# Encoder layer on one core: the first token group's finished rows go to memory and are normed in later chunks; its difference forms are made in the output projection and loaded in order of use; row loads are spread over the side steps

## The chip, the core and the metric

The kernel runs on one core of a Trainium2 chip. The metric is the device time of one execution in microseconds, as the median of several runs. The engines are TensorE (PE, with its weight loads as PEld), VectorE (DVE), ScalarE (ACT), GpSimd (POOL) and SyncE (SP), which here only issues DMAs. Each works through its own list of instructions in order.

## The reference

One encoder layer for 1536 tokens (512 of `x_prompt`, 1024 of `x_sample`), D = 1024, D_FF = 4096, all float32:

```python
x = x + merged @ w_out                        # output projection
h2 = rms_norm(x, g_mlp)
x = x + jnp.square(jax.nn.relu(h2 @ w_up)) @ w_down
return rms_norm(x, g_final)
```

`merged` is the gated sum of dilated-window attention and of a spatial-gating unit. That part comes first and the change doesn't touch it.

## The kernel before

Tokens lie in 12 tiles of 128. A float32 matrix product is made of three matmuls over values split in two: `split` (L149 to L151) has ScalarE cast the high part (`hi`, or `hf` and `act` for stationary and moving operands) and VectorE subtract it for the low part (`lo`). Weights come by SP's DMA into `raw` tiles of 256 KB and are split so.

*Output projection* (L757 to L787). For each half `ch` of the columns and each tile t: 24 matmuls with w_out, VectorE adds the result to x1[t] (L773), ScalarE sums squares (L231). In the second half x1[t] is also stored to `x1_scr` (SP, L776), `rstd_of` (L211 to L222) makes the root by nine small VectorE operations, two L782 scale the row to h, and in the midst of the next tile's matmuls `h_features` transposes h on TensorE (L741), multiplies by g_mlp on VectorE into `h2T` (L743, two buffers), and SP stores h2T to `h2_scr` (L746).

*MLP.* Two groups g of 6 tiles each (768 tokens, in two halves of HT = 384). Products are done by a scheme of seven block products, called forms: p1, p2 and q4 use blocks as they are, q3, q5, q6, q7 sums or differences of blocks. A group has CH = 8 chunks of the hidden dimension. A chunk has two `up_products` (j = 0, 1: seven forms of 12 matmuls 128x384, L883, in the order UP_ORDER = p1, q6, q7, p2, q5, q4, q3; p2 goes on in p1's PSUM bank and q3 in q5's) with the squared relu, and one `down_products` (seven forms, three tiles each, matmuls 128x512, L933), which adds into the rows x[0..5]. I call the 168 matmuls L883 of a chunk its up product and the 126 matmuls L933 its down product. In an up product ScalarE copies p1's bank to `p` (L888), and VectorE makes `v` = q6 - p (L891). In a down product `held["p", t]` (tag p, 3 buffers) and `z` (tag z, 2 buffers) hold such sums; L949 and L950 add z into rows on GpSimd, L952 adds q5, L956 p2 and L958 q3 on VectorE, and L960 adds p on GpSimd after q3.

The group's forms of h2 are four slabs `hf[k]`. Group 0's are made at the MLP's start: 16 parts loaded from `h2_scr` (L1067), 16 sums on VectorE and 28 splits, k after k. Group 1's difference forms are made as side steps in chunks 1 to 4 of group 0 (`diff_steps`) and stored to `form_scr`; all 28 are loaded as `raw_form` and split (`form_steps`) in group 0's last chunk. Side steps are small pieces of such work; `Side` pops one after each form of a product.

At the MLP's start and after the first up product of group 1, `load_rows` has GpSimd load the six row tiles x from `x1_scr` (L1052, 512 KB each). In that first up product of group 1, group 0's rows are finished by `final_steps(..., spread=True)`: 12 squares on ScalarE (L231), the root, 12 scalings on ScalarE (L1038), 12 multiplications by g_final on GpSimd (L1039), 12 stores to the outputs on GpSimd (L1040). Group 1's rows are normed on VectorE (`normed`, L234) at the very end.

A framework's scheduler writes each engine's list from the program's order and its own estimates, and adds the waits that dependences and reused buffers need. So the place of an instruction is seen only in the built program.

Of the kernel before, what the change touches and what calls it, by code (L numbers as in the profile page):

```python
# [46 lines left out]
SUM_ROWS = 8  # L47
EARLY = 2
DIFFS = ("q3", "q5", "q6", "q7")
UP_ORDER = ("p1", "q6", "q7", "p2", "q5", "q4", "q3")  # L50
# [56 lines left out]
def encoder_kernel(ctx: ExitStack, tc: tile.TileContext, a):  # L107
# [25 lines left out]
    gate_scr = [dram.tile([P, NTOK], F32, name=f"gate_scr{m}") for m in range(EARLY)]  # L133
    form_scr = dram.tile([len(DIFFS), 4, P, HT], F32, name="form_scr")
    h2_scr = dram.tile([KB, P, NTOK], F32, name="h2_scr")
# [118 lines left out]
    with ExitStack() as ph:  # L254
# [3 lines left out]
        vs = vpool.tile([P, NT, DM], F32, name="vs")  # L258
        vparts = const.tile([P, 2 * 32], F32, name="vparts")[:, :2 * NT].rearrange("p (t i) -> p t i", i=2)

# [475 lines left out]
    def h_features(t, halves):  # L736

        for i, h in enumerate(halves):
            pt = tp_tile()
            for b in range(4):  # L740
# [7 lines left out]
                in_=hT2.rearrange("p (k t) -> p k t", k=4))  # L748

    for ch in range(2):  # L750
        cols = slice(ch * 512, (ch + 1) * 512)
# [11 lines left out]
        for t in range(NT):  # L763
            acc = acc_tile()
            terms = token_terms(hT[t // 4], t, lambda k: tuple(x[:, 0, :] for x in w[k]))
            steps = product_steps(acc, [terms[k] for k in w])
            for _ in range(HSTEP):
                next(steps)
            if late:
                h_features(*late)  # L770
            for _ in steps:
                pass
            nc.vector.tensor_add(x1[t][:, cols], x1[t][:, cols], acc)  # L773
            square_sum(x_parts[t][:, ch:ch + 1], x1[t][:, cols], pp)
            if ch:
                nc.sync.dma_start(out=x1_scr[t * P:(t + 1) * P, :], in_=x1[t])  # L776
                rstd = rstd_of(x_parts[t])
                hs = []
                for i in range(2):
                    cs = slice(i * 512, (i + 1) * 512)  # L780
                    h = pp.tile([P, 512], F32, tag="h2", name="h2", bufs=2)
                    nc.vector.tensor_scalar(h, x1[t][:, cs], rstd, None, op0=ALU.mult)  # L782
                    hs.append(h)
                late = t, hs
        if late:
            h_features(*late)
# [128 lines left out]

    def down_products(act, c, x, ending):

        held = {}
        for form in ("p1", "q4", "q6", "q7", "q5", "p2", "q3"):
            w = [  # L920
# [43 lines left out]

    def diff_steps(k):

        x = {}

        def load(key, r, s):
            x[key] = unit("diff")  # L970
            nc.sync.dma_start(out=x[key], in_=h2_scr[4 * s + k, :, GT + r * HT:GT + (r + 1) * HT])

        def store(form, key):
            nc.sync.dma_start(out=form_scr[DIFFS.index(form), k], in_=x[key])

        def first():
            load("a", 0, 0)
            load("b", 1, 0)
            nc.vector.tensor_sub(x["a"], x["a"], x["b"])
            store("q7", "a")  # L980

        def second():
            load("c", 1, 1)
            nc.vector.tensor_sub(x["b"], x["b"], x["c"])
            store("q5", "b")

        def third():
            nc.vector.tensor_add(x["c"], x["a"], x["c"])
            store("q6", "c")

        def fourth():
            load("d", 0, 1)
            nc.vector.tensor_sub(x["d"], x["d"], x["c"])
            store("q3", "d")

        return [first, second, third, fourth]

    def form_source(form, k):
        if form in DIFFS:
            return form_scr[DIFFS.index(form), k]  # L1000
        r, s = {"p1": (0, 0), "p2": (0, 1), "q4": (1, 1)}[form]
        return h2_scr[4 * s + k, :, GT + r * HT:GT + (r + 1) * HT]

    def form_steps(fs):

# [3 lines left out]
        def step(i):  # L1009
            for j in range(i, min(i + 4, len(items))):  # L1010
                if j not in raws:
                    raws[j] = unit("raw_form")
                    nc.sync.dma_start(out=raws[j], in_=form_source(*items[j]))
            form, k = items[i]
# [3 lines left out]

    def final_steps(g, x, tiles, g_final, spread):

# [11 lines left out]
        def rows(j, i):  # L1032
            scale = found["rstd"][:, j:j + 1]
            r = x[tiles[j]][:, i * 512:(i + 1) * 512]
            y = y_rows[6 * g + tiles[j]][:, i * 512:(i + 1) * 512]
            gf = g_final[i]
            if spread:
                nc.scalar.activation(r, r, AF.Copy, scale=scale)  # L1038
                nc.gpsimd.tensor_mul(r, r, gf)  # L1039
                nc.gpsimd.dma_start(out=y, in_=r)  # L1040
            else:
                normed(r, r, scale, gf)
                (nc.scalar, nc.sync)[i].dma_start(out=y, in_=r)
# [4 lines left out]
    def load_rows(g):  # L1048
        x = {}
        for t in (3, 4, 5, 0, 1, 2):  # L1050
            x[t] = mp.tile([P, DM], F32, tag="x", name="x", bufs=6)
            nc.gpsimd.dma_start(out=x[t], in_=x1_scr[(6 * g + t) * P:(6 * g + t + 1) * P, :])  # L1052
        return x

    def gains():
        g_final = [mp.tile([P, 512], F32, tag="z", name="g_final", bufs=2) for i in range(2)]
        for i in range(2):
            load_g(g_final[i], a["g_final"][i * 512:(i + 1) * 512])
        return g_final


    hf = {k: Forms("hf") for k in (3, 0, 1, 2)}
    for k in range(4):
        parts = {}
        for s, r in ((0, 0), (0, 1), (1, 1), (1, 0)):
            parts[r, s] = unit(f"h{r}{s}")
            nc.sync.dma_start(out=parts[r, s], in_=h2_scr[4 * s + k, :, r * HT:(r + 1) * HT])  # L1067
        hf[k].put("p1", parts[0, 0])
        s2 = hf[k].sums(parts[0, 0], parts[1, 0], parts[1, 1])
        hf[k].put("q4", parts[1, 1])  # L1070
        hf[k].last(parts[0, 1], s2)
    x = None
    CH = DFF // P // 4
    for g in range(2):
        for c in range(CH):
            act = []
            final = c == CH - 1
            if g and not c:
                side.add([lambda: None] * 2 + final_steps(0, x, (3, 4, 5, 0, 1, 2), gains(), True))
            for j in range(2):  # L1080
                act.append(Forms("act"))
                if not g and final and j:
                    side.add(form_steps(hf))
                up_products(hf, 2 * c + j, act[j], lambda form: side(1 + (not c)))
            if not c:
                side.flush()
                x = load_rows(g)
            if not g and 1 <= c <= 4:
                side.add(diff_steps(c - 1))
            ending = None  # L1090
            if g and final:
# [3 lines left out]
                def ending(form, t):  # L1095
                    tiles = (3, 4, 5) if (form, t) == ("q5", 2) else (t,) if form == "q3" else ()
                    if tiles:
                        side.add(final_steps(1, x, tiles, [wide[:, :512], wide[:, 512:]], False))
                        side.flush()

            down_products(act, c, x, ending)
            if not g and final:
# [26 lines left out]
```

## Time and profile before

| | |
|---|---|
| median of 3 runs | 2782.21 us (2781.27 to 2785.49) |
| profiled execution | 2783.46 us, span 2781.7 us, mean granted TensorE clock 0.987 |
| busy: TensorE, VectorE, ScalarE, GpSimd | 2681.2 (96%), 1731.4 (62%), 1296.4 (47%), 392.3 us (14%) |
| DMA | 373.57 MB, 134 GB/s over the span |
| first matmul of the MLP, of group 1, last matmul's end | 1771.31, 2269.96, 2765.77 us |

Times in the rows are microseconds from the span's start. Where a row has an idle time in brackets, the arrow names who ended it.

### The profile page before, as it was taken

To read this page: it belongs to the slowest core of one execution; us is meant where nothing else is said; L and a number is where in the kernel's file an instruction comes from. 1 tells how busy PE (TensorE), PEld (TensorE's weight loads), DVE (VectorE), ACT (ScalarE), POOL (GpSimd) and SP (SyncE) were. 2 spreads that over 40 slices of the span, in tenths; PEclk is the share of its full clock that TensorE was granted. 3 is DMA by queue.
4 is the path that set the end of the run, shared out by engine and by line. 5 is a ranking of instruction groups with operands and counts; after the bars stand their busy time and mean duration, and the time that the engine had idled before them with its cause. 6 is when DMAs were issued, how large, how long until landed. Compare 5 with 4: busy or idle time off the path is not lost.

```text
span 2781.7 us, 38699 instructions
## 1 busy us (share of the span) xinstructions
PE 2681.2 (96%) x13400; PEld 2297.2 (83%) x13400; DVE 1731.4 (62%) x3665; ACT 1296.4 (47%) x2778; POOL 392.3 (14%) x418
## 2 busy tenths in 40 slices
PE   7999999999999999999999999699999978999997
PEld 5788888888888887888888888588889967998896
DVE  6542200166666666555555436688888887888887
ACT  5321111255566556553534321455555564665555
POOL 2000000011021212100000000022322134111321
PEclk9999999999999999999999999899999998999999
DMA  3112222237576767554444435545454455444443
GB/s 132 51 52 72 89 76 80 87 109 177 156 171 184 169 180 177 143 157 147 128 147 119 126 136 170 165 135 160 152 151 129 140 164 179 125 132 125 125 128 128
DMA packets 374516, 373.57 MB, mean 134 GB/s; under 512 B 21936, under 2 KB 294832, under 8 KB 370736
## 3 DMA queue, kind: packets, MB, share of 16 engines
q1 hardware_dynamic: 343344, 262.51, 31.4%
q0 software_dynamic: 21584, 66.90, 10.4%
q10 hardware_dynamic: 9392, 41.69, 4.5%
q8 instruction: 106, 1.74, 0.3%
q14 instruction: 90, 0.74, 0.1%
HBM read 321.95 MB, written 116.16 MB: 158 GB/s over the span
## 4 chain that ended last, share of the span: by engine, by line
PE 37%; DVE 8%; issue 5%; ACT 4%; DMA 3%; POOL 2%; SPq 0%; DVEq 0%; ACTq 0%; POOLq 0%
PE acc L933 9%; PE acc L175 7%; PE acc L176 7%; PE acc L177 7%; PE acc L883 6%; DVE lo L151 3%; DMA raw<-up_q 1%; ACT hi L150 1%; POOL x L950 1%; POOL x L949 1%; DVE act L151 1%; ACT a L870 1%; ACT a L871 1%; ACT act L150 1%; DVE x L958 1%
## 5 line engine op out<-in xcount | busy, mean ns | idle before, releaser
L151 DVE TENSOR_TENSOR lo<-raw,hi 128x512 fp32r<-128x512 f32 x694 | 545.1, 791 | 406.3 <-ACT hi L150 400.2
L150 ACT CAST hi<-raw 128x512 fp32r<-128x512 f32 x696 | 430.6, 620 | 647.0 <-PE acc L176 230.3
L175 PE MATMUL acc<-res_h,hi 128*128 128x512 f32 x1344 | 556.5, 414 | 0.8 <-DVE stg L576 0.8
L177 PE MATMUL acc<-res_h,lo 128*128 128x512 f32 x1344 | 526.8, 392 | 0.0
L176 PE MATMUL acc<-res_l,hi 128*128 128x512 f32 x1344 | 525.5, 391 | 0.0
L883 PE MATMUL acc<-hf,hi 128*128 128x384 f32 x1792 | 468.2, 342 | 42.0 <-ACT hf L150 16.8
L933 PE MATMUL acc<-hi,act 128*128 128x512 f32 x1344 | 420.2, 392 | 1.6 <-ACT hi L150 1.6
L883 PEld LDWEIGHTS acc<-hf,hi 128*128 128x128 f32 x1792 | 327.8, 191 | 56.7 <-ACT hf L150 20.6
L883 PE MATMUL acc<-hf,lo 128*128 128x384 f32 x896 | 303.4, 339 | 3.7 <-DVE lo L151 3.6
L933 PEld LDWEIGHTS acc<-hi,act 128*128 128x128 f32 x1344 | 254.3, 189 | 54.5 <-ACT hi L150 2.0
L177 PEld LDWEIGHTS acc<-res_h,lo 128*128 128x128 f32 x1344 | 252.6, 188 | 54.9
L175 PEld LDWEIGHTS acc<-res_h,hi 128*128 128x128 f32 x1344 | 254.1, 189 | 36.6 <-DVE stg L576 0.9
L176 PEld LDWEIGHTS acc<-res_l,hi 128*128 128x128 f32 x1344 | 254.5, 189 | 36.0
L933 PE MATMUL acc<-lo,act 128*128 128x512 f32 x672 | 264.7, 394 | 7.3 <-DVE lo L151 7.3
L548 ACT ACTIVATE pr<-pr,stg 128x128 f32<-128x128 f32 (+2 forms) x288 | 125.9, 438 | 177.1 <-DVE stg L545 140.7
L883 PEld LDWEIGHTS acc<-hf,lo 128*128 128x128 f32 x896 | 171.0, 191 | 5.2 <-DVE lo L151 5.2
L949 POOL TENSOR_TENSOR x<-x,z 128x512 f32<-128x512 f32 x48 | 71.2, 1484 | 623.0 <-DVE z L948 623.0
L933 PEld LDWEIGHTS acc<-lo,act 128*128 128x128 f32 x672 | 127.2, 189 | 37.0 <-DVE lo L151 10.7
L518 DVE TENSOR_TENSOR q<-qT,q 64x256 fp32r<-64x256 f32 x288 | 120.6, 419 | 48.0 <-ACT q L515 44.3
L560 DVE COPY pT<-tp 128x512 f32<-128x512 f32 (+1 forms) x144 | 82.1, 570 | 94.7 <-PE tp L558 93.7
L570 PEld LDWEIGHTS o<-v,pT 128*128 128x128 f32 x896 | 120.3, 191 | 25.0 <-DVE pT L560 14.7
L570 PE MATMUL o<-v,pT 128*128 128x64 f32 x896 | 117.3, 268 | 7.9 <-DVE pT L560 7.7
(183 smaller groups left out, 4081.8 us busy)
## 6 DMA issues: line engine op xcount, KB each, us to landing
raw<-in_w_in_dram SPq DMA_DIRECT2D x192, 256.0 KB, 3.1
raw<-up_q SPq DMA_DIRECT2D x128, 256.0 KB, 2.8
raw<-down_q SPq DMA_DIRECT2D x128, 256.0 KB, 2.7
raw<-in_w_up_dram SPq DMA_DIRECT2D x96, 256.0 KB, 2.8
raw<-in_w_down_dram SPq DMA_DIRECT2D x96, 256.0 KB, 2.8
up_q<-in_w_up_dram POOLq DMA_DIRECT2D x32, 512.0 KB, 9.2
down_q<-in_w_down_dram POOLq DMA_DIRECT2D x32, 512.0 KB, 10.4
raw<-in_w_branch_b_dram SPq DMA_DIRECT2D x48, 256.0 KB, 2.9
```

What stands on the lines that cost most here:

```text
L150: nc.scalar.copy(hi, src)
L151: eng.tensor_sub(lo, src, hi.bitcast(F32))
L175: nc.tensor.matmul(out, sh, mh, start=i == 0, stop=False)
L176: nc.tensor.matmul(out, sh, ml, start=False, stop=False)
L177: nc.tensor.matmul(out, sl, mh, start=False, stop=i == n - 1)
L518: nc.vector.tensor_sub(q2[rows, h, 1, :], src, q2[own, h, 0, :].bitcast(F32))
L548: last_of["act"] = nc.scalar.activation(pr[:, h, at:at + kn], pr[:, h, at:at + kn], AF.Exp, bias=low, scale=-1.0, accum_out=stg[:, j, 130 ...
L560: nc.vector.tensor_copy(self.pT[:, :n], pt[:, :n])
L570: nc.tensor.matmul(o[:, (2 * j + h) * 64:(2 * j + h + 1) * 64], self.pT[:, q * P:(q + 1) * P], found["v"][:, slot, h * 64:(h + 1) * 64], s ...
L883: nc.tensor.matmul(acc, st, mv, start=not on and k == 0 and n == 0, stop=k == 3 and n == 2, skip_group_check=bool(on))
L933: nc.tensor.matmul(acc, st, mv, start=not on and k == 0 and n == 0, stop=k == 1 and n == 2, skip_group_check=bool(on))
L949: nc.gpsimd.tensor_sub(x21, x21, z)
```

## The change

1. Group 0's difference forms are made in the second half of the output projection. After tiles 7 to 10 four steps each run (`SUMS_AT`): GpSimd loads parts of h2 into the rooms of x1[0..5], which are no longer needed, VectorE makes the sums, GpSimd stores them to `form_scr[0]`. At the MLP's start `form_steps(0, hf)` loads all 28 forms in the order of use.
2. Row loads go from GpSimd to SP and are side steps of the j = 1 half of a group's first up product (`load_steps`).
3. Group 0's finished rows are stored as they are to `row_scr` (GpSimd, six of 512 KB). In chunks 1 to 6 of group 1 `stored_steps(t)` loads one tile's row and g_final (four loads of 256 KB on GpSimd, in buffers of the tags p and z), takes its squares (ScalarE), its root and its norm (VectorE) and stores it (GpSimd).
4. In each group's last chunk the addition of p to a row (L960, now L997) comes right after q5, and group 1's last down product takes its forms in the order p1, q6, q7, q4, q5, p2, q3.

```diff
+SUMS_AT = {7: 4, 8: 4, 9: 4, 10: 4}
...
+    row_scr = dram.tile([GT, DM], F32, name="row_scr")
...
+    def diff_steps(g, k, new, eng):
+        def load(key, r, s):
+            x[key] = new()
+            eng.dma_start(out=x[key], in_=h2_scr[4 * s + k, :, g * GT + r * HT:g * GT + (r + 1) * HT])
+        def store(form, key):
+            eng.dma_start(out=form_scr[g][DIFFS.index(form), k], in_=x[key])
+        def first():
+            load("a", 0, 0); load("b", 1, 0); load("c", 1, 1); load("d", 0, 1)
+            nc.vector.tensor_sub(x["a"], x["a"], x["b"])
+            store("q7", "a")
...
+    for k in range(4):
+        room = [x1[(2 * k + i // 2) % 6][:, i % 2 * HT:(i % 2 + 1) * HT] for i in range(4)]
+        sums += diff_steps(0, k, lambda room=room: room.pop(0), nc.gpsimd)
...
+                for _ in range(SUMS_AT.get(t, 0)):
+                    sums.pop(0)()
...
-        for form in ("p1", "q4", "q6", "q7", "q5", "p2", "q3"):
+        for form in ("p1", "q6", "q7", "q4", "q5", "p2", "q3") if last else ("p1", "q4", "q6", "q7", "q5", "p2", "q3"):
...
+    def stored_steps(t):
+        def load():
+            for i in range(2):
+                cs = slice(i * 512, (i + 1) * 512)
+                r.append(mp.tile([P, 512], F32, tag="p", name="row", bufs=3))
+                nc.gpsimd.dma_start(out=r[i], in_=row_scr[t * P:(t + 1) * P, cs])
+                gf.append(mp.tile([P, 512], F32, tag="z", name="g_final", bufs=2))
+                load_g(gf[i], a["g_final"][cs])
+        def squares():
+            parts = row_parts()
+            junk = mp.tile([P, 512], F32, tag="p", name="junk", bufs=3)
+            for i in range(2):
+                nc.scalar.activation(
+                    junk, r[i], AF.Square, scale=HALF_MEAN, accum_out=parts[:, i:i + 1])
...
+        return [load, nothing, nothing, squares, nothing, root, lambda: rows(0), lambda: rows(1)]
+    def load_steps(g, x):
+        def load(t):
             x[t] = mp.tile([P, DM], F32, tag="x", name="x", bufs=6)
-            nc.gpsimd.dma_start(out=x[t], in_=x1_scr[(6 * g + t) * P:(6 * g + t + 1) * P, :])
+            nc.sync.dma_start(out=x[t], in_=x1_scr[(6 * g + t) * P:(6 * g + t + 1) * P, :])
...
-            if g and not c:
-                side.add([lambda: None] * 2 + final_steps(0, x, (3, 4, 5, 0, 1, 2), gains(), True))
+            if g and 1 <= c <= 6:
+                side.add(stored_steps(c - 1))
...
+                    tile_of = {"q5": 3 + t, "q3": t}.get(form)
+                    if tile_of is not None:
+                        nc.gpsimd.dma_start(out=row_scr[tile_of * P:(tile_of + 1) * P, :], in_=x[tile_of])
```

What it moves, at the places the prediction speaks of. First SP's list at the start of the MLP. `h_scr<-h2T` are the last stores of the output projection; before, the loads of h parts follow them, and the row loads are not on this engine:

```order
251 L156 DMA raw<-in_w_up_dram 128x4x128 x2
252 L776 DMA x_scr<-x_11_13954 128x1024
253 L746 DMA h_scr<-h2T 128x4x128 x4
254 L1067 DMA h_15121<-h_scr 128x384
255 L1067 DMA h_15123<-h_scr 128x384
```

After, on SP at the same place, with the forms (`raw_form`), the rows (`x<-x_scr`) and up weights (`raw`):

```order
252 L816 DMA x_scr<-x_11_13956 128x1024
253 L748 DMA h_scr<-h2T 128x4x128 x4
254 L1023 DMA raw_form<-h_scr 128x384 x4
255 L1023 DMA raw_form<-form_scr_95 128x384 x3
256 L1086 DMA x<-x_scr 128x1024 x2
257 L1023 DMA raw_form<-form_scr_95 128x384 x4
258 L158 DMA raw<-up_q_102 128x4x128
259 L1086 DMA x<-x_scr 128x1024
```

The row loads have come to SP, behind seven form loads; then a row stands about every fifth form.

Next the change of groups. Before, on GpSimd, behind the last additions of group 0's last down product:

```order
208 L960 TENSOR_TENSOR x<-x,p 128x512 x3
209 L1039 TENSOR_TENSOR x<-x,g_final 128x512
210 L1040 DMA out_y_prompt_dram<-x 128x512
211 L1039 TENSOR_TENSOR x<-x,g_final 128x512
212 L1040 DMA out_y_prompt_dram<-x 128x512
```

After, on GpSimd (L997 are the additions of p, L992 and L993 those of z):

```order
228 L997 TENSOR_TENSOR x<-x,p 128x512 x3
229 L992 TENSOR_TENSOR x<-x,z 128x512
230 L993 TENSOR_TENSOR x<-x,z 128x512
231 L992 TENSOR_TENSOR x<-x,z 128x512
232 L993 TENSOR_TENSOR x<-x,z 128x512
233 L992 TENSOR_TENSOR x<-x,z 128x512
234 L993 TENSOR_TENSOR x<-x,z 128x512
235 L1128 DMA row_scr<-x 128x1024 x6
```

The additions of p stand ahead of those of z, and six row stores take the place of the multiplications and output stores. On SP, after, at that place, where before only weights stood:

```order
439 L158 DMA raw<-in_w_up_dram 128x4x128
440 L1086 DMA x<-x_scr 128x1024 x3
441 L158 DMA raw<-up_q_102 128x4x128
442 L158 DMA raw<-up_q_101 128x4x128
443 L158 DMA raw<-in_w_up_dram 128x4x128
444 L158 DMA raw<-up_q_100 128x4x128
445 L1086 DMA x<-x_scr 128x1024
```

Row loads stand between the weights of p1 and q6 and between later ones.

Last, the norm in group 1, on ScalarE after, from the end of one down product's weights into the next up product (L1066 are the squares, L930 the copy of p1, L912 and L913 the squared relu of p2):

```order
1492 L152 CAST hi<-raw 128x512 x13
1493 L1066 ACTIVATE junk,parts<-row 128x512
1494 L930 COPY p_21008<-acc 128x384
1495 L152 CAST hi<-raw 128x512
1496 L1066 ACTIVATE junk,parts<-row 128x512
1497 L152 CAST hi<-raw 128x512 x3
1498 L912 ACTIVATE a_21078<-acc 128x384
```

And on GpSimd after, at the end of a down product (L1003 are the additions of p, L1058 the row's loads):

```order
243 L239 DMA g_final<-in_g_final_dram 128x512
244 L1003 TENSOR_TENSOR x<-x,p 128x512
245 L1058 DMA row<-row_scr 128x512
246 L1003 TENSOR_TENSOR x<-x,p 128x512
247 L1058 DMA row<-row_scr 128x512
248 L1003 TENSOR_TENSOR x<-x,p 128x512
249 L1075 DMA out_y_prompt_dram<-row 128x512 x2
```

The first square has come ahead of p1's copy, and two loads between the three additions, which stood in a row before. The tile of the row and the one that the square writes take turns in the three buffers of the tag p, so the square also waits for the third addition.

More of the change, by code (lines that the diff above doesn't have):

```diff
@@ L963, in down_products, with form_source, form_steps @@
                 side()
[L965 to L998, printed above, removed]
+    def form_source(g, form, k):
         if form in DIFFS:
-            return form_scr[DIFFS.index(form), k]
+            return form_scr[g][DIFFS.index(form), k]
         r, s = {"p1": (0, 0), "p2": (0, 1), "q4": (1, 1)}[form]
-        return h2_scr[4 * s + k, :, GT + r * HT:GT + (r + 1) * HT]
-    def form_steps(fs):
+        return h2_scr[4 * s + k, :, g * GT + r * HT:g * GT + (r + 1) * HT]
+    def form_steps(g, fs):
         items = [(form, k) for form in UP_ORDER for k in range(4)]
@@ L1017, in form_steps, with final_steps @@
         return [lambda i=i: step(i) for i in range(len(items))]
-    def final_steps(g, x, tiles, g_final, spread):
+    def final_steps(x, tiles, g_final):
         n = len(tiles)
@@ L1032, in rows @@
         def rows(j, i):
-            scale = found["rstd"][:, j:j + 1]
             r = x[tiles[j]][:, i * 512:(i + 1) * 512]
[L1035 to L1043, printed above, removed]
+            normed(r, r, found["rstd"][:, j:j + 1], g_final[i])
@@ L1055, in gains, with root, rows, nothing @@
[L1055 to L1071, printed above, removed]
+    def stored_steps(t):
+        r, gf, found = [], [], {}
+        def load():
[11 more added lines that the diff above has]
+                    junk, r[i], AF.Square, scale=HALF_MEAN, accum_out=parts[:, i:i + 1])
+            found["parts"] = parts
+        def root():
+            found["rstd"] = rstd_of(found["parts"])
+        def rows(i):
+            normed(r[i], r[i], found["rstd"], gf[i])
+            nc.gpsimd.dma_start(out=y_rows[t][:, i * 512:(i + 1) * 512], in_=r[i])
+        def nothing():
+            pass
+        return [load, nothing, nothing, squares, nothing, root, lambda: rows(0), lambda: rows(1)]
@@ L1072, in encoder_kernel @@
+    def load_steps(g, x):
+        def load(t):
+            x[t] = mp.tile([P, DM], F32, tag="x", name="x", bufs=6)
+            nc.sync.dma_start(out=x[t], in_=x1_scr[(6 * g + t) * P:(6 * g + t + 1) * P, :])
+        return [lambda t=t: load(t) for t in (3, 4, 5, 0, 1, 2)]
+    hf = [Forms("hf") for k in range(4)]
+    side.add(form_steps(0, hf))
     x = None
@@ L1082, in encoder_kernel @@
                 if not g and final and j:
[L1083 to L1087, printed above, removed]
+                    side.add(form_steps(1, hf))
+                if first and not j:
+                    side(4)
+                if not c and j:
+                    x = {}
+                    side.add(load_steps(g, x))
+                up_products(hf, 2 * c + j, act[j], lambda form: side(4 if first and not j else 1))
             if not g and 1 <= c <= 4:
-                side.add(diff_steps(c - 1))
+                side.add(diff_steps(1, c - 1, lambda: unit("diff"), nc.sync))
             ending = None
```

36 lines of the change are left out of this document (26 added, 10 removed).

## The prediction

> **What bounds the kernel now.** I read the page's slices first, then the stretches between the first matmuls of successive products, then the order in time around the two worst stretches. In the slices each digit is a tenth of busy time, and TensorE is full except at three places: the start of the MLP, the change of groups, and the end.
>
> ```profile
> PE   7999999999999999999999999699999978999997
> ```
>
> The second view gives busy time, granted clock and DMA for seven stretches (start and end in us). Rows 1 and 2 are the up products of the first group's chunks 0 and 1, row 3 its last down product, rows 4 and 5 the second group's first up and down products, row 6 an undisturbed up product (chunk 2), row 7 the last down product.
>
> ```profile
> 1771.31:1815.62 44.31, 39.15 (x169) 33.15 (x169) 38.89 (x78) 30.13 (x65) 0.00 (x0) 0.84 0.36 114
> 1844.22:1875.60 31.38, 29.70 (x170) 29.09 (x169) 25.47 (x42) 20.52 (x40) 4.69 (x3) 1.00 0.46 138
> 2228.55:2269.96 41.41, 34.13 (x130) 25.50 (x129) 38.55 (x64) 22.81 (x48) 11.41 (x9) 0.92 0.59 184
> 2269.96:2325.81 55.85, 35.24 (x168) 32.53 (x167) 41.13 (x55) 34.86 (x78) 28.45 (x33) 0.80 0.60 194
> 2325.81:2355.38 29.57, 29.57 (x128) 24.39 (x127) 23.40 (x38) 12.51 (x24) 8.90 (x6) 0.97 0.36 110
> 2414.14:2443.56 29.42, 29.42 (x169) 29.10 (x168) 24.22 (x40) 20.17 (x40) 4.70 (x3) 1.00 0.47 141
> 2734.63:2765.77 31.14, 29.33 (x127) 23.39 (x126) 25.30 (x49) 15.41 (x36) 13.00 (x9) 1.00 0.27 85
> ```
>
> An up product costs 29.42 us undisturbed. The one at the change of groups costs 55.85, the first of the MLP 44.31: 26.4 and 14.9 us too long. An undisturbed chunk is bound by TensorE with VectorE at 24.22 of 29.42 us (82%), so what is put into such chunks has 5.2 us of VectorE to fill.
>
> Order in time at the start of the MLP (start, duration, engine, operation; in brackets the idle time before and what ended it):
>
> ```profile
> 1752.82 2.67 POOL L1052 DMA_DIRECT2D x<-x_scr  x5 [32.29 <-DVE h L782]
> 1757.20 1.34 PE L741 MATMUL tp<-ident,h 128*128 128x128 f32 x8 [3.50 <-DVE h L782]
> 1765.00 1.33 DVE L743 TENSOR_TENSOR h2T<-tp,g_mlp 128x512 f32<-128x512 f32 x2 [7.55 <-DMA h_scr<-h2T]
> 1771.31 1.28 PE L883 MATMUL acc<-hf,hi 128*128 128x384 f32 x2 [12.77 <-ACT hf L150]
> ```
>
> The last tile's h2T waits 7.55 us for a store to free its buffer, and that store shares the DMA with five row loads of 512 KB issued at 1752.82. Everything up to the first up matmul hangs on it.
>
> At the change of groups:
>
> ```profile
> 2266.30 0.97 SPq L156 DMA_DIRECT2D raw<-up_q  x2
> 2291.65 5.34 DVE L151 TENSOR_TENSOR act<-s,act 128x384 fp32r<-128x384 f32 x3
> 2299.73 9.28 DVE L151 TENSOR_TENSOR lo<-raw,hi 128x512 fp32r<-128x512 f32 x3
> 2299.99 2.50 POOL L1039 TENSOR_TENSOR x<-x,g_final 128x512 f32<-128x512 f32 x2
> 2309.40 0.68 DVE L151 TENSOR_TENSOR lo<-raw,hi 128x512 fp32r<-128x512 f32 x1
> 2315.96 0.62 ACT L150 CAST hi<-raw 128x512 fp32r<-128x512 f32 x1 [5.41 <-DMA raw<-in_w_up_dram]
> ```
>
> A `lo` takes 0.68 us alone, and three take 9.28 while GpSimd multiplies rows by g_final (L1039). Then ScalarE waits 5.41 us for a weight.
>
> **The change, part by part**, against the profiled execution's 2783.46 us (span 2781.7), which is 1.25 above the median of 2782.21.
>
> 1. *Hand-over to the MLP.* The row loads leave GpSimd's queue, and SP issues them behind the first seven form loads, so no row load meets the last h2T stores. The 7.55 us go: **-7.55**, between -7.6 and -4 if one store still lands late. Next late is the 3.50 us wait for the norm, which stays; the first up matmul comes at about 1763.8.
>
> 2. *The MLP's first up product.* Sixteen loads become 28, and the 16 VectorE sums go. The DMA's rate:
>
> ```profile
> GB/s 12 0 310 300 228 306 57 149 360 414 408 417 403 371 97 74 268 250 324 302 293 21 141 146 248 37 92 107 299 74 0 0 0 0 0 0 112 79 206 193
> h<-h_scr SPq DMA_DIRECT2D x16, 192.0 KB, 3.2
> x<-x_scr POOLq DMA_DIRECT2D x5, 512.0 KB, 8.0
> 1760.00:1780.00 20.00, 7.24 (x19) 5.00 (x19) 9.46 (x20) 5.98 (x13) 0.00 (x0) 0.54 0.72 235
> ```
>
> From about 1759.5 (a form's load takes 3.2 us and its split 1) to the product's end come 28 x 192 KB of forms, 6 x 512 of rows and 14 x 256 of weights: 12,032 KB or 12.3 MB. At 235 GB/s (the mean of the hand-over's 20 us) that lasts 52 us, at 410 (its four best slices) 30 us: the end lies between 1795 (1763.8 + 29.4, and about 2 of cold clock) and 1813. VectorE's 38.89 us shrink by 16 x 0.55 = 8.8 to 30, so it is no longer what holds it. I take 1803, the middle, since ten of the slices, 1.4 us each, run above 300: 39 us instead of 44.31, **-5** (-13 to +5). The next chunk, 31.38, comes nearer the others: **-1**.
>
> 3. *Difference forms in the output projection.* Sixteen adds of 128x384, with GpSimd's loads and stores (16 each of 192 KB).
>
> ```profile
> 1700.00:1725.40 25.40, 25.40 (x130) 21.34 (x129) 17.15 (x57) 2.90 (x8) 0.57 (x1) 1.00 0.53 181
> 1771.77 0.55 DVE L817 TENSOR_TENSOR s<-h,h 128x384 f32<-128x384 f32 x1
> ```
>
> Four tiles take 25.40 us there, and VectorE is busy 17.15: 2.06 us free a tile. The adds stand in two groups of eight, each in one tile's time: 8 x 0.55 = 4.4 us, 2.3 too much, twice 4.7. What doesn't fit is made up in the tiles behind, unless TensorE runs out of banks. **+2.7**, between 0 and +6.
>
> 4. *Last down product of the first group* (41.41 us, VectorE busy 38.55). GpSimd's three adds of p (about 1.5 us each) move ahead, into VectorE's full stretch; the `lo` rows above show VectorE held beside GpSimd. **+1.5**, between 0 and 3 x 1.5 = +4.5.
> The Trainium skill, SBUF — State Buffer, section "Who interferes with whom", says that a VectorE instruction with two SBUF inputs contends with a GpSimd instruction that reads SBUF, and that the loser blocks fully. The trace agrees (9.28 us for three). By that rule the term would be the whole 4.5, and the sum 3 less of a gain.
>
> 5. *Change of groups.* Twelve squares and twelve scalings on ScalarE, twelve multiplications and twelve stores on GpSimd leave. Six row stores of 512 KB on GpSimd come, and on SP three row loads in front of the second form's weight, each waiting for its row store to land. VectorE's last add for them ends at 2261.7, and transfers of that size take 5.7 to 8.0 us, so SP is past the three near 2270.5; the weight was issued at 2266.30 before. It lands 2.8 us later and is split 1.3 us after that, at 2274.6; TensorE wants it 12 matmuls into the product, at 2272.1. I take 29.5 + 2.5 = 32 us for 55.85: **-24**, between -27 (no wait) and -16 (the other three rows hold up a weight each). The down product behind it loses its 1 us: **-1**.
>
> ```profile
> raw<-up_q SPq DMA_DIRECT2D x128, 256.0 KB, 2.8
> 2261.06 0.67 DVE L952 TENSOR_TENSOR x<-x,acc 128x512 f32<-128x512 f32 x1
> 2300.00:2320.00 20.00, 12.29 (x58) 11.97 (x58) 12.62 (x9) 5.99 (x12) 11.07 (x14) 0.76 0.88 297
> x<-x_scr POOLq DMA_DIRECT2D x6, 512.0 KB, 5.7
> ```
>
> The clock (0.76) sank there with TensorE's idle time, and is part of the 24.
> The Trainium skill, TensorE: Matmul & The Clock Gate, Part 1, has the clock halve after an idle window of about 3.4 us and recover after as much sustained work. These rows fit. By it a 2.5 us wait leaves the clock whole, and a first product that stops for every form runs at half clock time and again: that is the second rival's ground.
>
> 6. *Stored rows normed in chunks 1 to 6 of the second group.* Each chunk gets four loads, two squares, nine small VectorE operations, two scalings and two stores. What counts is where they stand. The first square stands in ScalarE's order ahead of the copy of p1, and it writes the third p buffer, which GpSimd's third add of p frees. On that copy waits the p2 form, which goes on in p1's bank 36 matmuls into the product.
>
> ```profile
> 2414.47 4.70 POOL L960 TENSOR_TENSOR x<-x,p 128x512 f32<-128x512 f32 x3 [5.00 <-DVE x L958]
> 2417.38 0.47 ACT L888 COPY p<-acc 128x384 f32<-128x384 f32 x1
> 1753.65 0.63 ACT L231 ACTIVATE junk<-x 128x512 f32<-128x512 f32 x1 [4.24 <-DVE x L773]
> 1754.18 0.19 ACT L231 ACTIVATION_READ_ACCUMULATOR junk<-x 128x1 f32 x1
> 1754.67 0.15 DVE L211 SCALAR_TENSOR_TENSOR rs_v<-xp 128x1 f32<-128x1 f32 x1
> ...
> 1756.38 0.16 DVE L222 SCALAR_TENSOR_TENSOR rs_y<-rs_u,rs_y 128x1 f32<-128x1 f32 x1
> 2294.73 0.54 POOL L1040 DMA_DIRECT2D out_y_sample_dram<-x  x1
> out_y_sample_dram<-x POOLq DMA_DIRECT2D x4, 256.0 KB, 2.5
> 2419.64 0.55 DVE L891 TENSOR_TENSOR v<-acc,p 128x384 f32<-128x384 f32 x1
> 2765.54 4.06 DVE L234 SCALAR_TENSOR_TENSOR x<-x,rs_y,g_final 128x512 f32<-128x512 f32 x6
> ```
>
> In chunk 2, which starts at 2414.14, the adds run from 0.33 to 5.03 us. Two load issues of 0.54 now stand between them: the third ends at 6.1. The first row, asked for at 1.9 and landing within 2.5 to 3.5, is there before. The square and its accumulator take 0.82, the copy 0.47: it ends at 7.4. p2 wants it at 36 x 0.174 = 6.25: TensorE waits about 1.2 us in each of six chunks, 7.2 us. VectorE waits there too (its v came at 5.5 before), and its new work (two scalings at 4.06/6 = 0.68, and the root chain, 1.87 from first to last) brings it from 24.2 to 27.5 of 30.6 us; for that I add 0.3 a chunk. **+9**, between +3 (the adds come earlier) and +20 (3.3 us a chunk: all the new VectorE work ends on the path).
>
> 7. *Last chunk.* q6 and q7 come earlier, so GpSimd's adds end before q5 needs them:
>
> ```profile
> 2759.51 0.69 DVE L952 TENSOR_TENSOR x<-x,acc 128x512 f32<-128x512 f32 x1 [1.25 <-POOL x L950]
> 2761.58 0.50 PE L933 MATMUL acc<-hi,act 128*128 128x512 f32 x1 [1.59 <-ACT hi L150]
> ```
>
> Of 1.25 and 1.59 us I count half, since the squares that hold the `hi` cast stay: **-1.5**, between -3 and +1.
>
> Sum: -7.55 - 5 - 1 + 2.7 + 1.5 - 24 - 1 + 9 - 1.5 = -26.85. From 2783.46 that is 2756.6, from the median 2755.4. I say 2756.
>
> **Rivals.**
> - *Norms take more of it.* VectorE without slack spreads each delay over the chunk: term 6 at +20 gives 2767. For it: 82% before the new work. Against it: nothing of it stands in down products, where VectorE has 23.40 of 29.57. Chance 0.18.
> - *The first product is paced by its loads.* The rows aren't spread far: they stand between the form loads and delay them. Then it ends at 1813, term 2 is +5 and the sum 2766. For it: 235 GB/s; against it: 410. Chance 0.13.
> - *More is won.* The first product ends at 1795 (-13) and the norms cost 3: 14 better, 2742. For it: ScalarE has 9 us free per up product. Chance 0.16.
> - *Slower.* One mechanism: the row that the first square wants lands late, and ScalarE, in order, holds the p1 copy and TensorE behind it. Without term 6 the gain is 35.9 us; it is used up at 6.0 us a chunk, so the copy would end 12.25 us into the product, and the row land at 11.0, 9.1 us after its issue; from 7 us a chunk the kernel is 0.2% slower, 2789. For it: 512 KB loads took 8.0 us at the hand-over. Against it: 256 KB ones on this queue took 2.5. Chance 0.08, of which 0.03 within 0.2%.
>
> **How the numbers follow.** The forecast has 0.45, with its own range 2748 to 2764. Faster by over 0.2% (5.6 us, about what this measurement can tell from no change): 0.45 + 0.18 + 0.13 + 0.16 = 0.92, from which I take 0.01 for unnamed mishaps. Slower 0.05, same 0.04. The range 2738 to 2773 takes in the second and third rival's ends and the first's.
>
> **What would show it.** VectorE's 7.55 us wait at h2T gone, and the first up matmul about 11 us after the last w_out matmul; the group-change up product near 32 us with no 9 us `lo` and clock near 1.0; in chunks 1 to 6 a TensorE wait on the p1 copy of about 1.2 us, up products of 30.9. Wrong would be an up product there above 33 us, or a first product above 44.

## The result, and the profile after

The changed kernel takes 2807.15 us (median of 4 runs, 2804.71 to 2807.75) against 2781.74 before: the ratio is 1.0088, 95% interval 1.007 to 1.0105. It is slower by 25 us where 2756 was forecast. Its profiled execution took 2806.87 us (span 2805.0), 23.3 more in span than the one before.

The stretches that answer to those shown of before: the first chunk of group 0 with both its products (72.91 us before, from 1771.31 to 1844.22), the last down product of group 0, the first up and down products of group 1, its up products in chunks 1, 2 and 6, and the last down product. Columns: stretch, length, busy time of TensorE, its weight loads, VectorE, ScalarE and GpSimd, granted clock, DMA share and GB/s.

```profile
1771.03:1843.98 72.95, 68.35 (x294) 57.08 (x295) 57.60 (x100) 43.62 (x88) 9.82 (x6) 0.88 0.60 194
2229.35:2277.53 48.18, 37.12 (x129) 27.09 (x128) 40.87 (x65) 23.11 (x50) 16.17 (x14) 0.86 0.67 223
2277.53:2311.39 33.86, 31.36 (x166) 30.30 (x167) 22.45 (x40) 20.74 (x41) 0.71 (x2) 0.95 0.68 212
2311.39:2339.99 28.60, 28.60 (x127) 23.65 (x127) 25.66 (x37) 12.05 (x23) 9.64 (x8) 1.00 0.44 118
2339.99:2378.16 38.17, 32.62 (x170) 31.84 (x168) 27.10 (x52) 22.36 (x45) 6.05 (x7) 0.91 0.49 146
2406.76:2441.73 34.97, 31.52 (x169) 30.59 (x168) 27.48 (x53) 21.64 (x44) 6.08 (x7) 0.95 0.53 158
2665.14:2699.17 34.03, 29.97 (x169) 29.03 (x168) 26.05 (x52) 21.63 (x44) 6.10 (x7) 1.00 0.56 164
2758.08:2789.09 31.01, 29.33 (x127) 23.39 (x126) 26.47 (x49) 15.30 (x36) 14.20 (x9) 1.00 0.25 85
```

The first up product of group 1 came near its forecast: 33.86 us where 32 was forecast and 55.85 stood before. The up products of chunks 1 to 6, which took 29.4 to 30.2 us each, now take 34.0 to 38.2. Laid over the prediction's terms (differences of the two traces; plus is longer):

| term | forecast, us | measured, us |
|---|---|---|
| 1 hand-over, last addition of the projection to first up matmul | -7.55 | -7.0 (18.4 to 11.4) |
| 2 first chunk; the chunks behind it | -5; -1 | 0.0; +1.0 |
| 3 output projection (its last addition) | +2.7 | +6.7 |
| 4 last down product of group 0 | +1.5 | +6.8 |
| 5 first up product of group 1; its down product | -24; -1 | -22.0; -1.0 |
| 6 up products of chunks 1 to 6 | +9 | +38.0 (178.2 to 216.2) |
| 7 last chunk and the end | -1.5 | +0.8 |
| sum | -26.85 | +23.3 |

So 29 of the 50 us between forecast and result lie in term 6. Both of the prediction's own signs of being wrong are there: the up products of these chunks are above 33 us, and the MLP's first up product is above 44 (46.5 from its first matmul to its last, nine matmuls of the down product among them). Who made TensorE wait in the six chunks (us in total, times, longest), in the view of waits, first before, then after:

```profile
PE acc L883 <- ACT p L888: 1.5, 4, 0.7
PE acc L925 <- ACT p L930: 24.0, 12, 5.4
PE acc L925 <- DVE a L943: 3.5, 5, 1.7
```

The place is the one the prediction named, ScalarE's copy of p1 (L930). Its size isn't. In order of time around the start of chunk 2's up product (2406.76), three engines together:

```profile
2400.44 0.56 POOL L239 DMA_DIRECT2D g_final<-in_g_final_dram  x1 [1.31 <-issue]
2403.60 0.69 DVE L995 TENSOR_TENSOR x<-x,acc 128x512 f32<-128x512 f32 x1 [3.14 <-POOL x L993]
2408.58 1.29 POOL L1003 TENSOR_TENSOR x<-x,p 128x512 f32<-128x512 f32 x1 [4.15 <-DVE x L1001]
2410.16 0.55 POOL L1058 DMA_DIRECT2D row<-row_scr  x1 [0.30 <-POOL x L1003]
2414.22 0.63 ACT L1066 ACTIVATE junk<-row 128x512 f32<-128x512 f32 x1 [3.96 <-POOL x L1003]
2414.85 0.46 ACT L930 COPY p<-acc 128x384 f32<-128x384 f32 x1
2415.36 0.61 PE L925 MATMUL acc<-hf,hi 128*128 128x384 f32 x2 [2.17 <-ACT p L930]
```

Read upward: TensorE waits 2.17 us for the copy; the copy stands behind the square; the square waits 3.96 us for GpSimd's third addition of p. The first of these additions starts 1.82 us into the product (0.33 before), since it waits for VectorE's q3 additions, which were late because VectorE had stood 3.14 us for GpSimd's last addition of z, in front of which GpSimd had issued a load of g_final. VectorE's waits for the additions of z around the start of this product, before and after:

```profile
DVE x L952 <- POOL x L950: 1.8, 2, 1.2
DVE x L995 <- POOL x L993: 3.7, 2, 3.1
```

From the first addition's start to the square's it is 5.64 us, as the prediction had it (0.33 to 6.1, 5.8). What it had wrong is that the chain starts at 0.33: in the six chunks it starts at 5.15, 1.82, 3.10, 3.61, 3.30 and 1.25 us (before, at 1.18 in the first and at 0.33 in the others).

Most of the rest of the loss is the clock. The same chunk in three stretches of 3.4 us, the first with the wait in it:

```profile
2412.90:2416.30 3.40, 1.23 (x7) 0.94 (x6) 0.44 (x1) 1.61 (x4) 1.28 (x1) 0.96 0.77 215
2416.30:2419.70 3.40, 3.40 (x13) 3.40 (x12) 2.54 (x11) 1.99 (x5) 0.00 (x0) 0.54 0.31 86
2419.70:2423.10 3.40, 3.40 (x21) 3.40 (x20) 3.31 (x8) 2.33 (x5) 1.06 (x2) 1.00 0.55 161
```

Behind the wait the clock is 0.54 for one stretch, and 13 matmuls run there instead of 21. Over chunks 1 to 5 some 63 matmuls ran at a spacing of 0.32 us for 0.173, which is 9 us.

### The profile page after: what moved, and what is told of

The parts are those of the page before. It is cut to its first block, busy times and chain, and to the rows that moved or that the text cites. A ratio compares the mean times of both kernels' runs of the same rounds, so it can differ in the third digit from the quotient of the medians.

```text
span 2805.0 us, 38877 instructions
## 1 busy us (share of the span) xinstructions
PE 2694.9 (96%) x13400; PEld 2305.9 (82%) x13400; DVE 1735.3 (62%) x3719; ACT 1290.3 (46%) x2766; POOL 397.2 (14%) x454
## 5 line engine op out<-in xcount | busy, mean ns | idle before, releaser
L925 PE MATMUL acc<-hf,hi 128*128 128x384 f32 x1792 | 474.6, 346 | 49.1 <-ACT p L930 28.3
L992 POOL TENSOR_TENSOR x<-x,z 128x512 f32<-128x512 f32 x48 | 71.2, 1483 | 573.0 <-DVE z L991 572.8
```

Source lines behind the costliest of these rows:

```text
L925: nc.tensor.matmul(acc, st, mv, start=not on and k == 0 and n == 0, stop=k == 3 and n == 2, skip_group_check=bool(on))
L992: nc.gpsimd.tensor_sub(x21, x21, z)
```

## The experiments

Medians stand beside the runs of the kernel before on the same chips (2781.7 to 2784.5); the column of up products is the sum over chunks 1 to 6 of group 1 in the profiled execution. That of e5 took 2784.43 us, 7 less than its median: three of its seven executions took 2781 to 2785 and four about 2792.

| run | median, us | ratio to before, 95% interval | up products, us |
|---|---|---|---|
| before; changed | 2781.74; 2807.15 | 1; 1.0088 (1.007 to 1.0105) | 178.2; 216.2 |
| e1 squares behind p1's copy | 2799.41 | 1.0056 (1.0037 to 1.0075) | 204.0 |
| e2 no norm | 2772.88 | 0.9958 (0.9943 to 0.9973) | 178.6 |
| e3 no norm, no sums in the projection | 2765.81 | 0.9937 (0.9922 to 0.9952) | 177.7 |
| e4 e1, rows on GpSimd, additions back | 2801.10 | 1.0062 (1.0047 to 1.0077) | 210.1 |
| e5 e1, all loads late | 2791.79 | 1.0019 (1.0006 to 1.0033) | 195.5 |
| e6 e1, g_final late | 2780.26 | 0.9986 (0.9977 to 0.9995) | 188.8 |
| e7 e1, rows late | 2786.48 | 1.0011 (1.0002 to 1.0021) | 193.4 |
| e8 e5, other places mended | 2785.64 | 1.0007 (0.9998 to 1.0016) | 196.7 |
| e9 e1, loads staggered | 2781.12 | 0.9994 (0.9985 to 1.0003) | 188.8 |
| e10 e9, no sums in the projection | 2776.07 | 0.9973 (0.9964 to 0.9983) | 190.9 |
| e11 e9, group 0's rows late | 2779.71 | 0.9987 (0.9977 to 0.9996) | 188.7 |
| e12 e10, group 0's rows late | 2777.25 | 0.9986 (0.9976 to 0.9995) | 189.7 |

**e1, the squares behind the copy.** The step moves two places later in the program, and a copy of a value of form q4 into the squares' result makes them depend on that form:

```diff
+            nc.scalar.copy(parts, act[0].slab[:, 0, FORMS.index("q4"), 0:2].bitcast(F32))
             junk = mp.tile([P, 512], F32, tag="p", name="junk", bufs=3)
...
-        return [load, nothing, nothing, squares, nothing, root, ...]
+        return [load, nothing, nothing, nothing, nothing, squares, nothing, root, ...]
```

> Same work and same DMAs as the changed kernel; only the squares of the stored rows are tied to a value of form q4 of the chunk (a 128x2 copy on ScalarE into their result first), so that they come behind the copy of p1 in ScalarE's list. Theory A (order): the 38 us that chunks 1 to 6 lost come from the copy of p1 waiting behind a square that waits for GpSimd's third add. Then these up products fall from 34.0-38.2 to 29.5-31 us and the kernel to 2770-2778 us. Rival B (load): VectorE and ScalarE are too full there (27 of 29.4 us), or the rows' DMAs hold the weights up. Then the up products stay above 33.5 us and the kernel above 2795.

It gave 2799.41, and the up products 204.0: theory A explains 12 of the 38 us, no more (the medians differ by 8). In the view of waits TensorE's chief releaser is now another:

```profile
PE acc L925 <- DVE a L943: 18.0, 6, 3.7
PE acc L925 <- ACT p L930: 2.8, 6, 0.6
```

The copy no longer counts, and VectorE is late instead: its addition a (L943) frees the bank of q5, in which q3 goes on. The additions of p still start 1.26 to 3.62 us into the product, so VectorE's list, which holds the q3 additions that they wait for, starts the product late as before. The time is the one that B expected (over 2795); whether for B's reason, e6 tells.

**e2, no norm; e3.** In e2 the rows go to the output unnormed, so it gives a price and is no kernel to use:

```diff
-            if g and 1 <= c <= 6:
-                side.add(stored_steps(c - 1))
...
-                        nc.gpsimd.dma_start(out=row_scr[...], in_=x[tile_of])
+                        nc.gpsimd.dma_start(out=y_rows[tile_of], in_=x[tile_of])
```

> Group 0's rows are stored to the output as they are and never normed: no row loads, squares, roots, scalings or second stores in chunks 1 to 6; all else as in the changed kernel. Prices all of that work: theories A and B both expect 2769 us (2807 less 38) with up products of 29.4-30.2; if those stay above 31, the loss has another cause than the norms. The distance to the run with the squares behind the copy is what the norms cost once they hold nothing: A expects 2-8 us, B over 25.

2772.88, and chunk 2's up product is back where it was:

```profile
2403.05:2432.48 29.43, 29.42 (x169) 29.10 (x168) 24.21 (x40) 20.25 (x40) 4.69 (x3) 1.00 0.48 141
```

The norm's place and work cost 37.6 us of up products, which is term 6 but for 0.4 us. Without the norm the change gains 0.4%.

e3 restores the start of the MLP (16 parts, sums there). Unlike what its expectation says, the kernel that ran also leaves the norm out, so it is to be read against e2, not against the changed kernel.

> Group 0's forms are made at the MLP's start from 16 parts as before (sums there, k after k), with the row loads still on SP as side steps; the rest as in the changed kernel. Theory A: the sums in the output projection cost the 6.7 us by which its last add moved, and bought nothing in the first up product: 2800 us, last add of the projection about 20 us before the MLP less the 7 us wait, first up product 44 again. Rival C: the order of forms and loads did help the first up product, by as much as the projection lost: 2805-2809.

2765.81, 7.1 below e2: theory A's difference, not C's. The projection's last addition is at 1754.23 (1762.32 in e2), and the first chunk takes 76.0 us for 73.8. The sums in the projection cost 8.1 and bring 2.2. The cost repeats: from the twelfth-last addition of the projection to its last it is 74.3 to 76.7 us in all nine kernels with the sums and 67.7 to 67.8 in the five without. The gain is within what the first chunk differs among kernels with the same start (71.6 to 75.3 us in eight with the sums).

**e4, three places mended at once.**

```diff
-            nc.sync.dma_start(out=x[t], in_=x1_scr[...])
+            (nc.gpsimd if g else nc.sync).dma_start(out=x[t], in_=x1_scr[...])
...
-                    if ending:                      # after q5
+                    if last:
                         nc.gpsimd.tensor_add(x12, x12, held["p", t])
```

> The squares behind the copy of p1, group 1's row loads on GpSimd's queue behind the row stores instead of SP's, and the additions of p in group 0's last down product back behind q3. Theory A with D (SP stood still for the row stores to land, so the next weight was late by 3.2 us on TensorE, and the moved additions cost 1 to 2): 4 to 6 us below the run with the squares alone, 2766-2773 us, the last down product of group 0 at 41-43 us instead of 48. Rival E: row loads on GpSimd's queue run into the weights' loads again, and the first up product of group 1 grows from 33.9 to over 38: no better than the squares alone, 2773-2780.

2801.10, not better than e1. The last down product of group 0 fell to 44.50 us (48.18; 45.3 to 49.2 in the eleven kernels that leave its lists as changed), the up product behind it grew to 39.26 (33.86). ScalarE waits there for weights again:

```profile
2275.44:2314.70 39.26, 33.02 (x166) 31.67 (x167) 24.50 (x40) 21.02 (x41) 5.40 (x8) 0.91 0.63 195
2289.22 2.12 ACT L152 CAST hi<-raw 128x512 fp32r<-128x512 f32 x3 [5.89 <-DMA raw<-up_q]
```

Rival E is what happened, but for its time, which was reckoned from an e1 at 2773 to 2780. Together the two products are 83.8 us for 82.0 (79.3 to 83.6 in the same eleven): the row loads cost no less on GpSimd's queue than on SP's.

**e5, e6, e7, the norm's loads.** From e1; in e5 all four loads are tied to form p1 of the chunk by a tiny copy into each tile, so that they come after GpSimd's additions; in e6 only the g_final loads, in e7 only the rows.

```diff
+                nc.scalar.copy(gf[i][:, 0:2], act[0].slab[:, 0, FORMS.index("p1"), 0:2].bitcast(F32))
                 load_g(gf[i], a["g_final"][i * 512:(i + 1) * 512])
...
+                nc.scalar.copy(r[i][:, 0:2], act[0].slab[:, 0, FORMS.index("p1"), 0:2].bitcast(F32))
                 nc.gpsimd.dma_start(out=r[i], in_=row_scr[...])
```

> Base: the changed kernel with the squares behind the copy (2799.4 us; without any norm 2772.9). Now also all four loads of a chunk's norm are tied to a value of form p1 of the chunk (128x2 copies on ScalarE into the tiles first), so that GpSimd issues them after the last of its additions; same work, same DMAs, four tiny copies more. Theory F (GpSimd's queue): what is left of the loss comes from DMA issues that stand between GpSimd's additions and make VectorE, which adds to the same rows behind them, late at the start of each up product. Then the up products of chunks 1 to 6 are 29.5-30.5 us and the kernel 2774-2780. Rival B (load): VectorE at 27.6 of 29.4 us is too full wherever the loads stand: up products stay above 32, the kernel above 2790.

> As the run with all loads late, but the two row loads stand between the three additions of p again; only the g_final loads come late. Under F it tells which of the two places costs more. F with the additions of z as the dearer place (VectorE's q5 adds wait for the third pair of them): 2778-2786. F with the additions of p as the dearer place: 2788-2797. B: 2795-2800.

> The other half: the row loads come late, the g_final loads stand between the additions of z again. F with z as the dearer place: 2788-2797; F with p: 2778-2786; B: 2795-2800. If both halves lie near the base, a single issue between additions already costs all.

2791.79, 2780.26 and 2786.48; up products 195.5, 188.8 and 193.4. Each half helps alone (15 and 11 us off the 204.0 of e1), the z side more; e6 lies where F put it with z as the dearer place, e7 between F's two ranges. With the g_final loads moved (e6) the additions of p start at 0.33 to 0.43 us in all six chunks, and TensorE's waits for VectorE's a fall to half of e1's; with only the rows moved (e7) they start at 1.3 to 3.6, as in e1. So the g_final loads are what made the chain start late:

```profile
PE acc L925 <- DVE a L943: 9.0, 12, 1.8
```

Both halves together gave less than either, which F didn't foresee. e5's trace, though of one of its faster executions, tells why, in its chunk 2 (ScalarE, then TensorE):

```profile
2420.32 0.63 ACT L1074 ACTIVATE junk<-row 128x512 f32<-128x512 f32 x1 [2.79 <-DMA row<-row_scr]
2425.21 0.73 PE L925 MATMUL acc<-hf,hi 128*128 128x384 f32 x2 [3.01 <-ACT p L930]
```

Four loads at once, and the row lands 5.9 us after its issue; the square waits for it, and p1's copy of the chunk's second half stands behind the square. It is the first fault again, half a product later.

**e8, the other places with e5.**

```diff
+            if g:
+                nc.scalar.copy(x[t][:, 0:2], act[0].slab[:, 0, FORMS.index("q4"), 0:2].bitcast(F32))
+            (nc.scalar if g else nc.sync).dma_start(out=x[t], in_=x1_scr[...])
```

with e3's start and e4's additions.

> All loads of the norm late and the squares behind the copy; group 0's forms made at the MLP's start as before; the additions of p in group 0's last chunk behind q3 as before; group 1's row loads issued by ScalarE in the middle of the first up product, tied to form q4, instead of SP between the weights. From the run with the loads late: less 7 (sums, as the runs without norm show: 2772.9 against 2765.8), less 6 to 8 (group 0's last down product and the next up product, 82 us together, to 74-76): 2760-2768. Rival: the row loads only move their cost behind, the two products stay at 80 or more: 2768-2774.

2785.64: the rival's case, but not its time, which was reckoned from an e5 at 2774 to 2780. The two products at the change of groups stay at 82.4 us, and the down product behind them takes 32.7 for 28.6, with 2.2 us of TensorE's waits for casts in it.

**e9 to e12, staggered.** In e9 the row loads are tied to p1's copy (about 5 us into the product), the g_final loads to form p1, the squares to q4; e10 is e9 with e3's start. In e11 and e12 ScalarE issues group 0's rows in the middle of the first up product, so that none stands between the form loads.

> Base: the run with all loads late (c1 to c6 up products 31.1 to 34.1, together 195.5 us; without norm 178.6). There the square of a row waited 2.8 us for a row that landed 5.9 us after its issue, four loads at once, and p1's copy of the second half stood behind it. Now the two row loads are tied to p1's copy of the first half (issued right behind the additions, about 5 us into the product), the g_final loads to form p1 (11 us), the squares to form q4 (14 us) as there. If ScalarE waiting for a late row is what was left (theory G), the rows are there when the squares come: up products 29.5-30.3 each, together 177-182, kernel 2773-2779. If VectorE's share (27 of 29.4 us) is what was left (B): up products stay at 31 or more, together over 186, kernel above 2780.

> The same, with group 0's forms made at the MLP's start as before instead of in the output projection. Less 7 us, as the two runs without norm differ (2772.9, 2765.8): 2766-2772 under G, above 2773 under B; and in the trace the last addition of the projection back where it was before the change (1752.9 instead of 1759.6).

e9 took 2781.12 with up products of 188.8, e10 2776.07. All six chunks of e9 have the clock at 1.00 and 30.9 to 31.9 us: better than e5, but not the 29.5 to 30.3 of theory G; that is B's number. It is also e6's: with the g_final loads out of the way, moving the rows too brought nothing more. What is left, 10 us in six chunks, shows in e9's waits, and in chunk 2 on ScalarE:

```profile
PE acc L925 <- DVE a L944: 9.0, 12, 1.5
2413.17 0.62 ACT L152 CAST hi<-raw 128x512 fp32r<-128x512 f32 x1 [2.58 <-DMA raw<-up_q]
2416.48 0.58 PE L925 MATMUL acc<-hf,hi 128*128 128x384 f32 x2 [0.56 <-DVE a L944]
```

A weight comes late while the rows load, the squared relu of p2 stands behind its cast, and VectorE's addition behind that. So in this half of chunk 2 it is the transfers more than VectorE's share; in the other half two parts of the norm (L236) stand in VectorE's list right before the addition. How the 10 us divide between the two was not measured.

> Base: the staggered run with the sums in the projection (2781). Only the six row loads at the MLP's start leave SP's list, where they stand between the form loads, and are issued by ScalarE in the middle of the first up product (tied to form q4 of its first half). If the first chunk, which got no shorter by the change (73.0 us from its first up matmul to the next chunk's, 72.9 before), is paced by its transfers (6 x 512 KB of 12.3 MB, at the 309 GB/s of its first 20 us: 10 us), it falls to 64-68 us and the kernel to 2772-2777. If what paces it is the splitting of 28 forms on ScalarE and VectorE and the cold clock, it stays at 71-73.

> The same with group 0's forms made at the MLP's start as before; base: 2776, where the first chunk took 75.6 us. Paced by transfers: 70 us or less, 2768-2772. Paced by the sums and splits in the order k after k: 74-76, no change.

2779.71 and 2777.25. The first chunk takes 71.4 us (73.0) in e11 and 77.6 (75.6) in e12. Among kernels with the same start the chunk differs by as much (71.6 to 75.3 in the eight with the sums, 74.3 to 76.0 in the three without), and the 64 to 68 of pacing by transfers is far off. So the rows between the form loads don't pace it; which of splits, cold clock and order does was not settled.

## Why the prediction was wrong

The step that failed is term 6: 29 of the 50 us between forecast and result. Terms 2, 3 and 4 are off by 7, 4 and 5.

1. *Hand-over*: right. -7.0 for -7.55, the store's wait is gone. The hand-over takes 11.2 to 11.6 us in all thirteen changed kernels, with and without the sums in the projection.

2. *First chunk*: wrong by 5, and the chunks behind it by 2. The estimate took the end from the transfers. e11 took a quarter of the bytes out of the way of the forms and gained 1.6, no more than the scatter. The second rival said that there would be no gain, but e11 speaks against its cause; what paces the chunk stays open.

3. *Output projection*: too low by 4. The term counted VectorE's work (4.7 us too much) and not what its list waits for. VectorE, in order, stood for GpSimd's loads, and the norm of a tile behind them; TensorE then waited for h:

```profile
1742.63 0.56 DVE L768 TENSOR_TENSOR x<-x 128x384 f32<-128x384 f32 x1 [3.96 <-DMA x<-h_scr]
1747.50 1.94 PE L743 MATMUL tp<-ident,h 128*128 128x128 f32 x8 [4.53 <-DVE h L822]
1759.60 0.69 DVE L813 TENSOR_TENSOR x<-x,acc 128x512 f32<-128x512 f32 x1 [0.62 <-PE acc L179]
```

The rows are GpSimd's late load seen by VectorE, TensorE's wait for h, and the projection's last addition, which stood at 1752.87 before; until then TensorE waited for no h there. e3 against e2 confirms the size (8.1).

4. *Last down product of group 0*: too low by 5. A wait was missing that neither this term nor term 5 has. The first two matmuls of the next up product stand in TensorE's list before the last 15 of the down product (at 2271.68, and at 2266.00 before, where the table ahead of the prediction gives 2269.96, their third), so what they wait for falls here:

```profile
2265.17 0.38 SPq L158 DMA_DIRECT2D raw<-in_w_up_dram  x1
2265.83 4.85 SPq L1086 DMA_DIRECT2D x<-x_scr  x3
2271.01 0.62 ACT L152 CAST hi<-raw 128x512 fp32r<-128x512 f32 x1 [1.92 <-DMA raw<-in_w_up_dram]
2271.68 0.62 PE L925 MATMUL acc<-hf,hi 128*128 128x384 f32 x2 [3.25 <-ACT hi L152]
2276.61 1.34 ACT L152 CAST hi<-raw 128x512 fp32r<-128x512 f32 x2 [4.98 <-DMA raw<-up_q]
2256.95 0.80 PE L976 MATMUL acc<-lo,act 128*128 128x512 f32 x1 [4.06 <-DVE lo L153]
```

The 3.25 us (0.38 before) are for the cast of the up product's first weight, which SP issued ahead of the rows. It landed 5.75 us after its issue, where it took 2.87 before, with three row stores of 512 KB issued in the 2.4 us before it. Every one of the thirteen kernels with these stores has it so: the weight takes 5.4 to 6.6 us and TensorE waits 2.9 to 4.1 us, in e4 and e8 too, where SP has no row loads there. So the row stores hold up a weight, which the prediction left out. SP's wait for them, which term 5 charged with 2.5 us, held up the weights issued behind the rows (the 4.98 us are ScalarE's, for one of them), but TensorE, late by then, didn't stand for that one. Its waits for `lo` are 7.5 us in all for 6.8 before, and 7.1 to 7.2 in e4 and e8, which have the additions of p back behind q3; so the moved additions can be charged with less than 1 us, and the clock (0.86 for 0.92) makes the rest. Of the rule that the prediction cites there (the Trainium skill, SBUF — State Buffer, section "Who interferes with whom") the runs show no more than this for 4.7 us of additions: the full 4.5 that it would have made did not come.

5. *Change of groups*: right in what leaves, and close by luck in what stays, 33.86 for 32. The 2.5 us for a weight behind the rows were not spent here; TensorE waits 2.00 us for VectorE's a (L943) and 0.38 for a cast instead, and the clock is 0.95.

6. *Norm in chunks 1 to 6*: the step that failed, +38 for +9. The mechanism (square before p1's copy, third addition of p) and the length of its chain were right. What failed is the chain's start, taken from the kernel before as 0.33 us into the product. The two g_final loads that stand between GpSimd's additions of z were read in the list and not priced: they make VectorE, and with it the additions of p, late, so that these start at 1.25 to 5.15 us (e6, with the loads moved: 0.33 to 0.43, and 15 us less than e1). Two costs come with it. VectorE's own list is late in the product, and q5's bank with it (e1: still 25 us above e2 with the copy out of the way). And a wait of about 2 us and more could set the clock back: 9 us, where the prediction had 2.5 us leave it whole. The "slower" rival had the right engine and the right total, 6 us a chunk, by luck: the row itself landed 3.5 us after its issue, as expected, and wasn't what the first square waited for. A late row did hold the copy, in e5. About 10 of the 38 us are left when all these places are mended (e9); whether VectorE's share, the first rival's ground, or the transfers make them is open.

7. *Last chunk*: 31.01 for 31.14, where -1.5 was forecast. The product takes 31.0 us in six of the thirteen changed kernels and 32.6 in seven, so no gain from the reordering of the forms shows.

The best version measured here that norms all rows is e10: 2776.07 us, ratio 0.9973 (0.9964 to 0.9983) to before. It keeps the stored rows, with the norm's steps tied to later values, and group 0's forms made at the MLP's start. The norm in chunks 1 to 6 still costs it about 10 us (its median against that of e3, which leaves the norm out; 13 in the up products of the two traces).

## What to carry to other kernels

Work that is moved into chunks which an engine's slack seems to hold is priced by where each of its instructions stands in each list, the DMA issues on a computing engine's list too: an issue between two additions costs whoever adds behind them (here the loads between the additions of z, e6 against e1). A step whose input comes late belongs behind everything short that others wait for; where the scheduler hoists it, a dependence on a later value puts it there (e1). When a chain decides, check its start as well as its length.

## What the runs showed of the hardware

A pause of TensorE of 2 to 4 us can halve the granted clock for the stretch behind it (0.54 in the result's table of three stretches). Six chunks of e5 run the same list; three had pauses of 2.9 to 3.1 us and a clock of 0.95, with 34 us, three had pauses of 1.6 to 1.9 us, a clock of 1.00 and 31 (one of each, columns as in the first table of stretches):

```profile
2401.21:2435.24 34.03, 31.02 (x170) 30.70 (x169) 26.25 (x51) 21.29 (x49) 7.95 (x9) 0.95 0.55 165
2463.84:2494.99 31.15, 29.41 (x169) 29.09 (x168) 26.13 (x51) 21.15 (x49) 7.96 (x9) 1.00 0.60 178
```

The length of the pause alone doesn't decide it. Over chunks 1 to 6 of all runs the shortest pause that was followed by about ten matmuls at 0.32 us spacing was 1.9 us (a chunk of e8; 2.0 in e7), and the longest that wasn't was 3.7 us (a chunk of e1); below 1.9 us none was. The Trainium skill, TensorE: Matmul & The Clock Gate, Part 1, has the clock fall after an idle window of about 3.4 us and says that the window runs free; a pause of 1.9 us is shorter than that, so the figure is no safe bound here.

A weight of 256 KB that SP issued behind three row stores of 512 KB landed 5.4 to 6.6 us after its issue in thirteen kernels, and 2.87 us in the kernel before, which has no such stores.

A DMA issue on GpSimd takes 0.55 us, and where it waits for the addition just before it, 0.30 us of idle time stand in front of it (22 rows of the changed kernel, the rows of the result's chunk among them). In three others, where the view names nothing that it waited for, it is 1.3 to 1.5 us.
